# Rotary embedding on one core: the tail of a load as a DMA of its own, and the first store behind the rest of that load

## Chip, core and metric

The kernel runs on one core of a Trainium2 chip, with no other core of this program at work. The metric is the device time of one execution in microseconds (us).

## What is computed

A rotary position embedding. The input has 16 batches, 512 positions and 16 heads of 64 numbers, all float32. In each head the first half x1 and the second half x2 are turned by tables that depend on the position alone:

```python
# x: [16, 512, 16, 64]; cos, sin: [512, 32]
x1, x2 = x[..., :32], x[..., 32:]
out = concatenate([x1 * cos - x2 * sin,
                   x1 * sin + x2 * cos], axis=-1)   # float32
```

33.55 MB come in and 33.55 MB go out; the two tables have 64 KB each.

## The kernel before

**Slabs.** The work is cut into 8 slabs of 2 batches, 4.19 MB each: 8192 float32 (32 KB) on each of 128 partitions. Two neighbouring slabs are one stretch of HBM, and a partition's part of the two is one row of 64 KB, so a load or store of two slabs at once (k = 2) moves 64 KB per partition, one of a single slab 32 KB. The tile `room` has place for six slabs. Slabs 6 and 7 take the places of slabs 0 and 1.

**Loads and stores.** `loads` and `stores` say which slabs go alone and which in pairs:

```python
loads = {0: 1, 1: 1, 2: 2, 4: 2, 6: 1, 7: 1}
stores = {0: 1, 1: 1, 2: 1, 3: 1, 4: 2, 6: 1, 7: 1}
```

The loads of slabs 0, 1, 2-3 and 4-5 are issued on SP's DMA queue at the very start, one behind the other (L73). The tables come by ACT's queue (L89). The loads of slabs 6 and 7 are issued by ACT in the middle of its work, and each waits until the store whose place it takes (store 0, store 1) has landed. All seven stores go out on SP's queue (L182), each when the last pass over its slab is done. Hence store 0 is issued while the load of slabs 4-5 is still on its way, and its bytes stand behind that load's in the same queue.

**Compute.** TensorE spreads the tables over the partitions with eight small matmuls (L130), and VectorE (DVE) copies them to bfloat16 (L135). Each slab is then one pass of 8192 numbers per partition, or two passes of 4096 (slabs 0, 6 and 7). In a pass ScalarE (ACT) casts float32 to bfloat16 in place (`cast`, L146), DVE makes two products (L174) and their sum (L177), and ACT casts the result back to float32 in place (L178). ACT's cast of the next pass stands ahead of this pass's cast back.

**What sets the order.** ACT's and DVE's instructions keep the order in which the program writes them (`manual_schedule`); so does SP's queue in effect: four loads, then the stores 0, 1, 2, 3, 4-5, 6 and 7. Waits on semaphores are put in by the framework from the data that instructions share.

Of the kernel before, what the change touches and what calls it, by code (L numbers as in the profile page):

```python
# [2 lines left out]

# [4 lines left out]


@with_exitstack  # L10
def kernel(
    ctx: ExitStack,
    tc: tile.TileContext,
    x: bass.AP,
    cos: bass.AP,
    sin: bass.AP,
    num_heads: int,
    out: bass.AP,
):
    nc = tc.nc  # L20
    P = nc.NUM_PARTITIONS

    batch, seq, dim = x.shape
    nh = num_heads
    hd = dim // nh
    half = hd // 2
    bf16 = mybir.dt.bfloat16
    f32 = mybir.dt.float32

    nb = 2  # L30
    slots = 6
    LATE = 3
    nslabs = batch // nb
    G = 2
    rpp = nb * seq // P
    W = rpp * dim
    SP = seq // rpp
    TW = rpp * half

    out_flat = out.rearrange("b s h d -> b s (h d)")  # L40

    singles = ctx.enter_context(tc.tile_pool(name="singles", bufs=1))
    psum = ctx.enter_context(tc.tile_pool(
        name="psum", bufs=1, space=bass.MemoryType.PSUM))


    def dram(t, s, k):
        return bass.AP(tensor=t.tensor,
                       offset=t.offset + s // G * (G * nb * seq * dim) + s % G * W,
                       ap=[[G * W, P], [1, k * W]])  # L50


    def view(t, offset, *dims):
        return dataclasses.replace(t, offset=t.offset + offset,
                                   ap=[t.ap[0], *[list(d) for d in dims]])


    room = singles.tile([P, slots * W], f32, tag="room")
    halves = room.bitcast(bf16)


    def slab(s, k):
        return view(room, s % slots * W, (1, k * W))


    loads = {0: 1, 1: 1, 2: 2, 4: 2, 6: 1, 7: 1}
    stores = {0: 1, 1: 1, 2: 1, 3: 1, 4: 2, 6: 1, 7: 1}


    def load(s):  # L70
        k = loads[s]
        queue = nc.sync if s < slots else nc.scalar
        queue.dma_start(out=slab(s, k), in_=dram(x, s, k))  # L73

    TR = 32
    TQ = seq // TR // rpp
    TC = seq * half // TR
    raw = singles.tile([P, TC], f32, tag="raw")  # L80
    nc.vector.memset(raw, 0.0)  # L81


    def load_tables(queue):
        for i, src in enumerate((cos, sin)):
            to = dataclasses.replace(
                raw, offset=raw.offset + i * raw.ap[0][0],
                ap=[[P // TR * raw.ap[0][0], TR], [1, TC]])
            queue.dma_start(out=to, in_=bass.AP(  # L89
                tensor=src.tensor, offset=src.offset, ap=[[TC, TR], [1, TC]]))  # L90


    load(0)
    load_tables(nc.scalar)
    for s in loads:
        if 0 < s < slots:
            load(s)

    GP = SP // G
    GT = G // TQ
    pick = singles.tile([P, 3 * GT * P], bf16, tag="pick")
    nc.gpsimd.memset(pick, 0.0)  # L104


    def selection(g, h):
        return pick[:, (g * GT + h // TQ) * P:(g * GT + h // TQ + 1) * P]


    for g in range(3):
        for h in range(0, G, TQ):
            part = view(selection(g, h), 0, (GP, P // GP), (1, GP))
            nc.gpsimd.affine_select(  # L114
                out=part, in_=part, compare_op=mybir.AluOpType.not_equal,
                fill=-1.0 if g == 2 else 1.0,
                base=-(1 if g else 0) - h // TQ * (P // TR),
                pattern=[[0, P // GP], [-(G // TQ) * (P // TR), GP]],
                channel_multiplier=1)

    raw_b = singles.tile([P, TC], bf16, tag="raw_b")
    nc.gpsimd.tensor_copy(out=raw_b, in_=raw)  # L122

    tab = {}


    def table(h):
        acc = psum.tile([P, 2 * rpp * hd], f32, tag=f"acc{h}")
        for g, at in ((0, 0), (0, half), (2, rpp * hd), (1, rpp * hd + half)):
            nc.tensor.matmul(  # L130
                view(acc, at, (hd, rpp), (1, half)), selection(g, h),
                view(raw_b, h % TQ * TW, (half, rpp), (1, half)),
                start=True, stop=True)
        tab[h] = singles.tile([P, 2 * rpp * hd], bf16, tag=f"tab{h}", name="tab")
        nc.vector.tensor_copy(out=tab[h], in_=acc)  # L135

    def span(u):
        s, r, n = u
        at, m = s % slots * W + r * dim, n * dim
        return (m, view(room, at, (1, m)), view(halves, 2 * at, (1, m)),  # L140
                view(halves, 2 * at + m, (1, m)))


    def cast(u):
        m, full, low, high = span(u)
        nc.scalar.copy(out=low, in_=full)  # L146

    passes = []
    for s in range(nslabs):
        n = rpp if 1 <= s < nslabs - 2 else rpp // 2
        passes += [(s, r, n) for r in range(0, rpp, n)]


    with tc.manual_schedule(engines={mybir.EngineType.Activation, mybir.EngineType.DVE}):
        cast(passes[0])
        done = 1
        for i, u in enumerate(passes):  # L160
            s, r, n = u
            if i == 0:
                for h in range(G):
                    table(h)
            ahead = len(passes[:rpp // passes[0][2]]) if i == 0 else i + 1
            for v in passes[done:ahead + 1]:
                cast(v)
            done = max(done, ahead + 1)
            if s - LATE + slots in loads and s >= LATE and r == 0:
                load(s - LATE + slots)  # L170
            m, full, low, high = span(u)
            turned = view(low, half, (hd, n * nh), (-half, 2), (1, half))
            for out_, in_, a in ((high, turned, rpp * hd), (low, low, 0)):
                nc.vector.tensor_mul(  # L174
                    out=out_, in0=in_,
                    in1=view(tab[s % G], a + r * hd, (hd, n), (0, nh), (1, hd)))
            nc.vector.tensor_add(out=high, in0=low, in1=high)  # L177
            nc.scalar.copy(out=full, in_=high)  # L178
            if r + n == rpp:
                for t, k in stores.items():  # L180
                    if t + k - 1 == s:
                        nc.sync.dma_start(out=dram(out_flat, t, k), in_=slab(t, k))  # L182


# [1 line left out]
_INS = ['x', 'cos', 'sin', 'num_heads']  # L186
_OUTS = [((16, 512, 16, 64), 'float32')]

_NUMBERS = {'num_heads': 16}


# [26 lines left out]
```

## Time and profile before

| | us |
|---|---|
| median of 3 runs | 162.21 (162.21 to 162.39) |
| the profiled execution | 162.0 |
| its span in the profile | 160.2 |

| engine | busy in the span |
|---|---|
| VectorE (DVE) | 110.1 us (69%) |
| ScalarE (ACT) | 113.2 us (71%) |
| TensorE (PE) | 1.9 us (1%) |
| GpSimd (POOL) | 2.1 us (1%) |

Some events of the span, from the trace:

| us | what |
|---|---|
| 0.74 to 2.8 | SP issues the loads of slabs 0, 1, 2-3 and 4-5 |
| 13.3, 22.9, 42.2 | the loads of slabs 0, 1 and 2-3 have landed, and ACT's casts begin |
| 36.93 | SP issues store 0 |
| 56.19 | SP issues store 1 |
| 62.5 | the load of slabs 4-5 has landed |
| 72.28 | store 0 has landed; ACT issues the load of slab 6 |
| 88.01 | store 1 has landed; ACT issues the load of slab 7 |
| 139.6 | the last cast back ends; SP issues store 7 |
| 159.3 | store 7 has landed |

An instruction that issues a DMA ends long before its bytes have landed; "landed" is when the semaphore of the DMA has its full count. All DMAs, of whichever queue, are carried by the same 16 DMA engines. "Packets" are the pieces in which an engine carries a DMA; here a packet is one partition's part (32 or 64 KB), eight of them per engine and DMA.

### The profile page before, as it was taken

Reading aid. Unit: us, or ns where it says so; the run is one execution under the profiler, and the core shown is the slowest. Engines: PE = TensorE matmul, PEld = TensorE weight load, DVE = VectorE, ACT = ScalarE, POOL = GpSimd, SP = SyncE. Lnnn points to the kernel's source line nnn. Section 1 sums busy time; section 2 is a strip of 40 time slices with the busy share of each in tenths; the row PEclk is TensorE's granted clock in tenths of the full one; section 3 lists DMA queues with packets and bytes.
Section 4 is the critical chain, followed back from the end, with each engine's and each line's share of the span. In section 5 each row is a group of like instructions: output and inputs, shape, how many; then the busy total and the mean of one; then the engine's idle time right before and its main releaser. Section 6 shows DMA issues by size and latency. Waiting matters only on the chain.

```text
span 160.2 us, 170 instructions
## 1 busy us (share of the span) xinstructions
PE 1.9 (1%) x8; PEld 1.1 (1%) x8; DVE 110.1 (69%) x36; ACT 113.2 (71%) x23; POOL 2.1 (1%) x9
## 2 busy tenths in 40 slices
PE   0004000000000000000000000000000000000000
PEld 0002000000000000000000000000000000000000
DVE  1002999999906998999899899997399999000000
ACT  3006939992499999999999999299999991800000
POOL 3001000000000000000000000000000000000000
DMA  7999999979989996999999999999998998999994
GB/s 262 409 409 393 515 401 524 458 327 524 425 360 524 409 376 270 458 450 401 458 450 393 450 466 393 442 442 425 417 532 360 524 409 376 401 458 450 393 442 213
DMA packets 1968, 67.24 MB, mean 420 GB/s; under 512 B 240, under 2 KB 240, under 8 KB 304
## 3 DMA queue, kind: packets, MB, share of 16 engines
q1 hardware_dynamic: 1584, 58.72, 85.8%
q10 hardware_dynamic: 384, 8.52, 12.3%
HBM read 33.69 MB, written 33.55 MB: 420 GB/s over the span
## 4 chain that ended last, share of the span: by engine, by line
ACT 36%; DMA 25%; DVE 21%; issue 4%; SPq 1%; ACTq 0%
DMA room<-in_x_dram 25%; ACT room L178 20%; ACT room L146 17%; DVE room L174 14%; DVE room L177 7%; SPq L73 1%; ACTq L178 0%
## 5 line engine op out<-in xcount | busy, mean ns | idle before, releaser
L174 DVE TENSOR_TENSOR room<-room,tab 128x4096 bf16<-128x4096 bf16 (+1 forms) x22 | 71.7, 3260 | 10.9 <-ACT room L146 10.5
L146 ACT CAST room<-room 128x4096 bf16<-128x4096 f32 (+1 forms) x11 | 56.6, 5155 | 17.1 <-DMA room<-in_x_dram 17.1
L178 ACT CAST room<-room 128x4096 f32<-128x4096 bf16 (+1 forms) x11 | 56.6, 5156 | 6.6 <-DVE room L177 6.6
L177 DVE TENSOR_TENSOR room<-room 128x4096 bf16<-128x4096 bf16 (+1 forms) x11 | 35.9, 3262 | 0.4
L135 DVE CAST tab<-acc 128x1024 bf16<-128x1024 f32 x2 | 2.4, 1219 | 13.6 <-PE acc L130 13.6
L146 ACT ACT_TABLE_LOAD x1 | 1.3, 1283 | 2.6 <-issue 2.6
L130 PE MATMUL acc<-raw_b,pick 128*128 128x256 bf16 x8 | 1.9, 415 | 13.9 <-POOL raw_b L122 13.9
L130 PEld LDWEIGHTS <-pick 128*128 128x128 bf16 x8 | 1.1, 140 | 14.2 <-issue 12.3
L81 DVE MEMSET raw<- 128x512 f32 x1 | 0.5, 485 | 0.9 <-PEq L199 0.9
L114 POOL TENSOR_SCALAR_AFFINE_SELECT pick<-pick 128x128 bf16<-128x128 bf16 x3 | 0.8, 309 | 0.1
L122 POOL CAST raw_b<-raw 128x512 bf16<-128x512 f32 x1 | 0.6, 611 | 11.2 <-DMA raw<-in_sin_dram 11.2
L104 POOL MEMSET pick<- 128x384 bf16 x1 | 0.4, 418 | 0.3 <-POOLq L199 0.3
L199 POOL MEMSET const-float32-0.0<- 128x1 f32 x1 | 0.1, 99 | 0.2 <-issue 0.2
L199 POOL MEMSET const-bfloat16-1.0<- 128x1 bf16 x1 | 0.1, 102 | 0.0
L199 POOL MEMSET const-uint8-127<- 128x1 uint8 x1 | 0.1, 102 | 0.0
L199 POOL MEMSET const-float32-1.0<- 128x1 f32 x1 | 0.1, 99 | 0.0
## 6 DMA issues: line engine op xcount, KB each, us to landing
out_dram<-room SPq DMA_DIRECT2D x6, 4096.0 KB, 33.6
room<-in_x_dram SPq DMA_DIRECT2D x2, 4096.0 KB, 17.1
room<-in_x_dram ACTq DMA_DIRECT2D x2, 4096.0 KB, 24.8
raw<-in_cos_dram ACTq DMA_DIRECT2D x1, 64.0 KB, 7.9
raw<-in_sin_dram ACTq DMA_DIRECT2D x1, 64.0 KB, 11.1
room<-in_x_dram SPq DMA_DIRECT2D x2, 50.5
out_dram<-room SPq DMA_DIRECT2D x1, 28.7
```

Source lines behind the costliest of these rows:

```text
L73: queue.dma_start(out=slab(s, k), in_=dram(x, s, k))
L81: nc.vector.memset(raw, 0.0)
L104: nc.gpsimd.memset(pick, 0.0)
L114: nc.gpsimd.affine_select(out=part, in_=part, compare_op=mybir.AluOpType.not_equal, fill=-1.0 if g == 2 else 1.0, base=-(1 if g else 0) - ...
L122: nc.gpsimd.tensor_copy(out=raw_b, in_=raw)
L130: nc.tensor.matmul(view(acc, at, (hd, rpp), (1, half)), selection(g, h), view(raw_b, h % TQ * TW, (half, rpp), (1, half)), start=True, sto ...
L135: nc.vector.tensor_copy(out=tab[h], in_=acc)
L146: nc.scalar.copy(out=low, in_=full)
L174: nc.vector.tensor_mul(out=out_, in0=in_, in1=view(tab[s % G], a + r * hd, (hd, n), (0, nh), (1, hd)))
L177: nc.vector.tensor_add(out=high, in0=low, in1=high)
L178: nc.scalar.copy(out=full, in_=high)
L199: nc = _bacc.Bacc("TRN2", target_bir_lowering=False, num_devices=1)
```

## The change

The load of slabs 4-5 becomes two DMAs on the same queue, one behind the other: the first 56 KB of each partition (14336 numbers), then the last 8 KB (2048 numbers, `TAIL` = 2 rows of 1024; 1.05 MB in all). Store 0 gets a wait: SP issues it only when the first of the two has landed. SP's order is now written out too (`manual_schedule` names SP), and stays as it was: five loads, then the seven stores. Nothing else is changed.

```diff
     slots = 6
+    TAIL = 2
...
+    gates = {4: 0}
+    opened = {}
+
+    def piece(t, s, a, b):
+        return bass.AP(tensor=t.tensor,
+                       offset=t.offset + s // G * (G * nb * seq * dim) + s % G * W + a,
+                       ap=[[G * W, P], [1, b - a]])
 
     def load(s):
-        k = loads[s]
+        end = loads[s] * W
+        cut = end - TAIL * dim if s in gates else end
         queue = nc.sync if s < slots else nc.scalar
-        queue.dma_start(out=slab(s, k), in_=dram(x, s, k))
+        for a, b in ((0, cut), (cut, end)):
+            if a < b:
+                done = queue.dma_start(
+                    out=view(room, s % slots * W + a, (1, b - a)),
+                    in_=piece(x, s, a, b))
+                if s in gates and a == 0:
+                    opened[gates[s]] = done.ins
+
+    def store(s):
+        gone = nc.sync.dma_start(out=dram(out_flat, s, stores[s]), in_=slab(s, stores[s]))
+        if s in opened:
+            tc.add_manual_dep(
+                gone.ins, opened[s].name,
+                mybir.DependencyInfo(mybir.DependencyClass.Sync,
+                                     mybir.DependencyReason.DATA),
+                reason="behind the load")
...
-    with tc.manual_schedule(engines={mybir.EngineType.Activation, mybir.EngineType.DVE}):
+    with tc.manual_schedule(engines={
+            mybir.EngineType.Activation, mybir.EngineType.DVE, mybir.EngineType.SP}):
...
-                        nc.sync.dma_start(out=dram(out_flat, t, k), in_=slab(t, k))
+                        store(t)
```

## The prediction

> **What bounds the kernel now.** I read the DMA row of the page first, then the stage table of the trace, then the starts of packets around the one stage that stands out, and last SP's waits. The page says that the 16 DMA engines carry the run:
>
> ```profile
> DMA  7999999979989996999999999999998998999994
> ...
> HBM read 33.69 MB, written 33.55 MB: 420 GB/s over the span
> ```
>
> The DMA row is full from the second slice to the last but one, while DVE and ACT are busy 69% and 71% and are done by 139.6 us. All 67.24 MB at the rate of the best stages (434 GB/s) would be 154.9 us of the 160.2. On SP's queue the waits say the same of the stores (us in total, times, longest): each was held until ACT's last cast (L178) of its slab, and its bytes then waited for the DMA engines.
>
> ```profile
> SPq L182 <- ACT room L178: 123.8, 7, 27.0
> ```
>
>  The chain of waits names ACT and DVE for most of the span, but after 139.6 us it has no instruction left to name and 20 us of stores are still to come, so the chain isn't the bound; the DMA engines are. Where do they run below 434? The stage table, with stages cut where packets begin (last column GB/s, the one before it the DMA share):
>
> ```profile
> 22.00:41.40 19.40, 0.00 (x0) 0.00 (x0) 19.26 (x7) 14.04 (x3) 0.00 (x0) 1.00 1.00 432
> 41.40:58.30 16.90, 0.00 (x0) 0.00 (x0) 11.87 (x4) 16.08 (x3) 0.00 (x0) 1.00 1.00 434
> 58.30:61.55 3.25, 0.00 (x0) 0.00 (x0) 3.25 (x1) 3.25 (x1) 0.00 (x0) 1.00 1.06 323
> 61.55:71.20 9.65, 0.00 (x0) 0.00 (x0) 9.12 (x3) 9.65 (x3) 0.00 (x0) 1.00 1.01 435
> 71.20:86.90 15.70, 0.00 (x0) 0.00 (x0) 15.10 (x5) 15.70 (x3) 0.00 (x0) 1.00 1.00 434
> 86.90:114.00 27.10, 0.00 (x0) 0.00 (x0) 23.46 (x7) 24.07 (x5) 0.00 (x0) 1.00 1.01 437
> ```
>
> One stage sticks out: 58.30 to 61.55 us, 323 GB/s though the DMA share is 1. It is the last packet that each engine carries of the load of slabs 4-5, with store 0 next on the same queue. The starts of packets in 53 to 63 us show it (40 slices of 0.25 us; GB/s is put down to the slice in which a packet begins):
>
> ```profile
> DMA  0099000000099600000009900000000000999009
> GB/s 0 0 3146 1049 0 0 0 0 0 0 0 786 3146 262 0 0 0 0 0 0 0 2359 1835 0 0 0 0 0 0 0 0 0 0 0 524 655 918 0 0 786
> ```
>
> Weighted means of the starts: 56.09, 58.48, then 61.92. The steps are 2.39 and 3.44 us, where a 64 KB packet takes 2.42 (packet records): the last packets of the load are stretched by 1.02 us. The landings agree. Loads 2-3 and 4-5 have 8.39 MB each; load 1 landed at 22.85, loads 2-3 at 42.20 and 4-5 at 62.5 (issued at 2.1, 60.4 to landing), so 19.35 and then 20.3 us: 1.0 us more. Nowhere else between 3.8 and 158 us is a packet stretched like this; start-up (first packets at 1.75 to 2.25 us, 2 us instead of 1.2) and the end after 158 us aren't touched by the change. So about 1.0 us, 0.6% of the run, is what the edit can play for.
>
> **The change part by part.** The profiled execution took 162.0 us, of which 160.2 is span and 1.8 lies around it; it is 0.2 below the median of the three runs (162.21). The terms below are differences of span, and I put them on the median.
>
> *The split.* On each engine, 8 packets of 64 KB become 8 of 56 KB and 8 of 8 KB. No 8 KB or 56 KB packet is in the trace; the nearest records are 2 KB (0.084 us), 32 KB (1.213) and 64 KB (2.418). They fit 0.008 us per packet plus 27.2 GB/s, so 2.12 and 0.309 us: 16.94 + 2.48 = 19.42 against 19.34. The price is +0.07 us. It lies on the path, as every microsecond of the queue does, and it has no cover. From below it can't be under 0; from above, the 2 KB packets' rate (24.4 GB/s) for the whole tail would make it 0.27. The SP issue of one DMA more (0.4 us by the rows at 1.2 to 2.1 us) ends by 3.3 us, long before the queue needs it: nothing.
>
> *The new wait.* The last packets of loads 2-3 end at 41.57 (mean), so those of the first part of load 4-5 end at 41.57 + 16.94 = 58.5, and the tail's at 61.0. A landing counter follows the last packet by 0.3 us (62.2 to 62.5), and SP adds an EVENT_SEMAPHORE and its restart (0.1), so store 0 is issued at about 59.0, not at 36.93. What happens from issue to first byte? For a store on a drained queue no row shows it; load 0 is the nearest: issued at 0.74, its packets begin at 1.75 to 2.25 (1.0 to 1.5 us later), and end at 3.8 on the mean, which without the latency would be a flow from 2.6 (1.85 later). The same load from its landing: 12.6 us, less 9.65 for its bytes at 434.5 GB/s, 0.3 for the 0.13 MB of tables between and 0.3 for the counter, leaves 2.15. So store 0 stands in the queue from 60.1 to 60.5 and could flow from 60.9 to 61.2, where the tail ends at 61.0. The gap is 0 to 0.2 us; I take 0, since load 0's latency includes HBM reads and a store reads the SBUF. With a tail half as long the gap would be 1.2 us more: the tail is all the cover there is.
>
> [...]
>
> *The stretch.* Its cause isn't in a row; the place is. It lies on the last packet of a load while packets of a store stand behind it on the same queue. Load behind load (at 22 and 41.5 us) and store behind store (71, 139) go on at 432 to 435, and from 76.7 to 114 us loads on the ACT queue alternate with stores on SP's packet by packet at 434 to 437, so the change of direction by itself is cheap. What is left is a store read ahead while the load ahead of it on its queue is unfinished, and that needs store 0 to be queued early. After the change nothing of it is there until 60.3 (mean), 0.7 us before the tail ends. Taken from both ends: if all goes, −1.02; if all stays, 0. Some stretch may come back in those 0.7 us: before, 1.02 of 3.44 us were lost (30%), so 0.2. I take −1.02 + 0.2.
>
> *What is queued behind it.* On SP store 1 (data ready at 56.19, issued then) now stands behind the waiting store 0 and goes out at about 59.5. Its turn in the queue is after store 0's last packet, near 70.7: covered by 10 us. Store 2 (70.03) isn't touched. ACT's issue of load 6 waits for store 0's landing (72.26 now) and sits in ACT's order between a cast that runs from 69.91 to 76.93 and the next; anywhere in it, the wait costs ACT nothing. Load 7 lies likewise in the cast from 83.75 to 90.77. The listing of the changed kernel has the same order on SP and ACT and one more counter in use, so some waits name another counter, each of a DMA long landed. ACT reads slab 5, where the tail lies, from 83.75, 22 us after it lands. At the end compute is done at 139.6 and the last store's turn comes at 149.3, so a shift of a microsecond changes nothing but the queue: what is won or lost near 61 us reaches the end whole.
>
> Sum: 162.21 − 1.02 + 0.2 + 0.07 = 161.46, say 161.5 us.
>
> **The rivals.** *The stretch belongs to the first store itself*, wherever it starts: every engine's first write to HBM, or the one switch from load to store on a queue. For it: the trace has only this one such switch, so there is no second sample. Against it: the load's landing is late, not the store's first packet (store 0 lands 9.7 us after that landing, its bytes' time being 9.65). Then the store arrives under the tail, the tail or the first store packet is stretched instead, and the run is 162.21 + 0.07 = 162.3, no change that can be seen (162.0 to 162.5). [...]
>
> *The store comes late, and the switch costs as before.* This one ends slower. The gap is what the 2.48 us tail doesn't cover of counter, SP, descriptors and first bytes; I have 0.3 + 0.1 + 1.85 to 2.15, so 2.25 to 2.55, with nothing to spare. ACT's load 6 shows a slower start on a busy engine: issued at 72.28, first packet on its queue after 76.7, 4.4 us, three 1.21 us packets of the other queue among them, so 0.8 us of it is start. If the start of a store on a drained queue is 0.5 us over load 0's, the gap is 0.5 to 0.6, and with the stretch unrelieved the run is 162.21 + 0.07 + 0.5 = 162.8 (162.55 to 163.2). It decides from the point where gap and remaining stretch together pass 1.02 − 0.07 + 0.32 = 1.27 us.
>
> *The edit does nothing at its place*: the stretch is due to something else at 58 us, as SP's issue of store 1 at 56.19. Other issues (36.93, 70.03, 125.46) left no mark, so I give it little, and it gives the first rival's time.
>
> **How the numbers follow.** A difference under 0.2% (0.32 us) can't be told from none here: the three runs spread over 0.18. Forecast, the stretch goes for the most part: 0.48, 161.5, its own range 161.2 to 161.9. Stretch stays, no gap, the third rival included: 0.23, 162.3. Gap and stretch: 0.29, 162.8. Range 161.2 to 162.9: from nothing left of the stretch to somewhat over the second rival's middle. Faster 0.48, same 0.23, slower 0.29.
>
> **What would show it.** In the profile after, the first part's landing near 58.8 and SP's issue of store 0 near 59.0; the starts of packets in 53 to 63 us with steps of 2.1, then small packets from 58.5, and store 0's first packets at 61.0 to 61.3 instead of 61.92. Store 0 landing near 71.5, not 72.26, and every later landing earlier by as much; span near 159.5. The first rival shows store 0's packets at 61.9 to 62.0 with no empty slice. The second shows DMA slices empty around 61 us and the landing of store 0 past 72.5. The forecast is wrong if store 0's first packets begin after 61.6.

## The result, and the profile after

| | before | changed |
|---|---|---|
| median of 22 runs each | 162.21 us (161.98 to 162.39) | 162.93 us (162.18 to 163.64) |
| ratio | | 1.0040 (95% interval 1.0031 to 1.0050) |
| the profiled execution | 162.0 us, span 160.2 | 163.36 us, span 161.6 |

The change makes the kernel slower by 0.4%, 0.72 us at the median. The runs also spread wider, 1.46 us against 0.41. The profiled execution of the changed kernel is one of its slower ones; a second trace of it (below) has 162.84 us. In the numbers of the experiments, runs over 1.5% above the fastest of the same kernel are left out (164.63 and 164.77 us of one_queue_wait, 164.50 of pair_no_wait2).

At the place that the change aims at, it did all it is for. SP's waits (us in total, times, longest) have store 0 held by the load now; its timeline has the issue of stores 0 and 1 one behind the other:

```profile
SPq L93 <- ACT room L205: 77.8, 5, 27.0
SPq L93 <- DMA room<-in_x_dram: 55.8, 1, 55.8
...
59.29 0.82 SPq L93 DMA_DIRECT2D out_dram<-room  x2
```

The starts of packets in 53 to 63 us, slices of 0.25 us as in the prediction:

```profile
DMA  0005995000009990000007899997999993039900
GB/s 0 0 0 229 1835 1376 229 0 0 0 0 0 459 2294 918 0 0 0 0 0 0 295 361 426 393 459 524 328 393 459 393 1475 655 131 0 131 1311 655 0 0
```

The 56 KB packets begin every 2.1 us. The 8 KB packets follow from 58.3 and each takes 0.31 us. Store 0's first packets (the 1475, 655 and 131) begin from 60.75 to 61.25, straight behind the tail: no stretch, no empty slice between. Store 0 landed at 71.41 us, 0.85 earlier than before.

The loss comes back later. These are rows of the stage tables (last column GB/s), the kernel before first, then the changed one; the stage from 74 to 89 us is that in which ACT's load of slab 6 cuts in between the stores:

```profile
61.55:73.60 12.05, 0.00 (x0) 0.00 (x0) 11.49 (x4) 12.05 (x3) 0.00 (x0) 1.00 1.01 435
73.60:88.50 14.90, 0.00 (x0) 0.00 (x0) 14.33 (x4) 14.90 (x3) 0.00 (x0) 1.00 1.01 435
88.50:157.00 68.50, 0.00 (x0) 0.00 (x0) 42.49 (x16) 44.47 (x11) 0.00 (x0) 1.00 1.00 433
```

```profile
60.75:73.90 13.15, 0.00 (x0) 0.00 (x0) 12.58 (x4) 13.15 (x3) 0.00 (x0) 1.00 1.02 442
73.90:89.00 15.10, 0.00 (x0) 0.00 (x0) 14.53 (x4) 15.10 (x3) 0.00 (x0) 1.00 1.02 404
89.00:157.00 68.00, 0.00 (x0) 0.00 (x0) 42.03 (x16) 44.11 (x11) 0.00 (x0) 1.00 1.00 433
```

435 became 404 GB/s there, with the DMA share at 1: packets took longer, up to 2.55 us for 32 KB where the usual one takes 1.213. I measure this by an *excess*: the time of each packet record over 0.008 us plus its bytes at 27.2 GB/s, summed and divided by 16 engines (to about 0.03 us). Before, it is 1.02 us at 55 to 66 us and nothing after; changed, 0.02 at 55 to 66 and 1.32 after, on store packets near 75.4 us, and on load packets near 77 and from 84 to 87 us.

It is also uneven. The last stage, second by second (the first two rows are the kernel before, the other two the changed one):

```profile
158.00:159.00 1.00, 0.00 (x0) 0.00 (x0) 0.00 (x0) 0.00 (x0) 0.00 (x0) 1.00 0.01 0
159.00:160.20 1.20, 0.00 (x0) 0.00 (x0) 0.00 (x0) 0.00 (x0) 0.00 (x0) 1.00 0.00 0
```

```profile
158.00:159.00 1.00, 0.00 (x0) 0.00 (x0) 0.00 (x0) 0.00 (x0) 0.00 (x0) 1.00 0.31 131
159.00:160.20 1.20, 0.00 (x0) 0.00 (x0) 0.00 (x0) 0.00 (x0) 0.00 (x0) 1.00 0.07 27
```

Before, no packet of data begins after 158 us. In the changed kernel four begin between 158 and 159 (131 GB/s, four of 32 KB) and one after 159. By the records the 16 engines end at 158.72 us on the mean and 159.01 at the latest before, 159.14 and 160.41 after. The mean engine is 0.42 later and the last one 1.40, and the kernel ends with the last. That is the span's 1.35 us.

### The profile page after: what moved, and what is told of

Same layout as the page of the kernel before. It is cut to its first block, busy times and chain, and to the rows that moved or that the text cites. A ratio compares the mean times of both kernels' runs of the same rounds, so it can differ in the third digit from the quotient of the medians.

```text
span 161.6 us, 173 instructions
## 1 busy us (share of the span) xinstructions
PE 1.9 (1%) x8; PEld 1.1 (1%) x8; DVE 110.1 (68%) x36; ACT 113.3 (70%) x23; POOL 2.1 (1%) x9
## 4 chain that ended last, share of the span: by engine, by line
ACT 36%; DMA 25%; DVE 21%; issue 4%; SPq 0%; ACTq 0%
DMA room<-in_x_dram 25%; ACT room L205 20%; ACT room L172 16%; DVE room L201 14%; DVE room L204 7%; SPq L85 0%; ACTq L205 0%
```

## The experiments

Each was timed in turns with the kernel before on the same chip. "Excess" is that of the profiled execution, in us, from 3 to 66 us of the span and from there to its end.

| kernel | median us (range) | ratio to before (95%) | excess, 3 to 66 us / after |
|---|---|---|---|
| before | 162.21 (161.98 to 162.39) | | 1.03 / 0 |
| changed | 162.93 (162.18 to 163.64) | 1.0040 (1.0031 to 1.0050) | 0.06 / 1.32 |
| split_only | 162.14 (162.00 to 162.36) | 1.0001 (0.9992 to 1.0010) | 1.42 / 0 |
| wait_only | 164.79 (164.56 to 165.88) | 1.0180 (1.0154 to 1.0206) | 0.10 / 1.41 |
| tail3 | 162.44 (161.87 to 163.30) | 1.0016 (1.0000 to 1.0031) | 0.74 / 0.05 |
| tail4 | 162.16 (162.01 to 162.31) | 0.9998 (0.9989 to 1.0007) | 1.12 / 0 |
| store_head | 162.13 (162.04 to 162.33) | 0.9995 (0.9987 to 1.0004) | 1.19 / 0 |
| store0_on_act | 162.39 (162.26 to 162.56) | 1.0011 (1.0002 to 1.0019) | 1.31 / 0 |
| one_queue_wait | 162.82 (162.10 to 164.01) | 1.0051 (1.0026 to 1.0075) | 0.02 / 1.48 |
| one_queue_free | 162.78 (162.57 to 163.17) | 1.0041 (1.0029 to 1.0053) | 1.33 / 0.32 |
| three_waits | 162.21 (161.62 to 163.77) | 1.0007 (0.9984 to 1.0030) | 0.20 / 0.62 |
| pair_no_wait2 | 162.73 (162.05 to 163.77) | 1.0027 (1.0008 to 1.0046) | 0.55 / 1.35 |
| pair_free | 162.51 (162.30 to 162.78) | 1.0019 (1.0010 to 1.0028) | 1.37 / 0.18 |
| pair_wait | 161.61 (161.28 to 162.03) | 0.9963 (0.9950 to 0.9977) | 0.03 / 0.42 |

Up to 0.4 us of the first figure lies between 30 and 50 us in some traces (tail3, pair_no_wait2, pair_free), on packets of the load alone; no run here tells why. The nomix pair, which is shorter, has its times below.

The theory, M: an engine loses about 1 us where load and store packets first meet in it, once; a kernel that is spared this at the first store pays later.

### One half of the change at a time

```diff
-        if s in opened:            # split_only: store 0 waits for nothing but its data
+        if False and s in opened:
-    TAIL = 2                       # wait_only: no split, store 0 waits for the whole load
+    TAIL = 0
```

> The split stays, the wait goes: store 0 is issued at 37 us again and stands behind the 8 KB tail on SP's queue. Theory M (about 1 us is lost where load and store packets first meet in the DMA engines; the wait moves the meeting from 58 us to the first load on ACT's queue near 75 us, where it costs more and unevenly between engines): the meeting is back near 58 to 62 us, later packets are whole, time as before plus 0.1 for the split, 162.1 to 162.4. Rival S (the small packets or the fifth load make the run slower): slow as the changed kernel, 162.9, with stretched packets after 75 us.

> The wait stays, the split goes: store 0 waits for the whole load of slabs 4-5. M: no stretched packet at 58 us, an empty queue of 1.4 to 2.1 us after 61 us, and the same loss of 1 us or more after 75 us as in the changed kernel: 164.2 to 165.0. Rival S: the gap alone on top of before less the stretch, 162.6 to 163.3.

Starts of packets in split_only, 53 to 63 us:

```profile
GB/s 0 0 0 0 918 2294 459 0 0 0 0 0 0 2294 1376 0 0 0 0 0 0 33 426 426 164 295 229 98 295 164 328 131 197 262 459 393 1081 1180 131 0
```

The tail begins at full rate (426) and then falls to half, 100 to 330 a slice, until about 61.2 us. By the records its 8 KB packets take 0.31 us at first, about 0.6 in the slow part, and 0.31 again from 61.2 us on; store 0's first packets begin only after that, from 62.13 to 62.51. The fifth load and its small packets cost nothing that the timing can tell (ratio 1.0001); rival S falls. In wait_only the queue runs dry. A row of the stage between the load and the store, and SP's issue of stores 0 and 1:

```profile
61.00:62.20 1.20, 0.00 (x0) 0.00 (x0) 1.20 (x1) 1.20 (x1) 0.00 (x0) 1.00 0.00 0
61.66 0.82 SPq L93 DMA_DIRECT2D out_dram<-room  x2
```

Store 0 goes out at 61.66 us and its first packets begin at 62.5, 0.85 us later. The gap is 1.6 us in the mean of the engines, and the excess after 66 us (1.41) is that of the changed kernel. So the tail covers the gap in full, and the later loss comes with the wait, with or without a split. The time at which load 6 is issued doesn't explain it: 71.49 us in the changed kernel and 72.84 in wait_only, which have the loss, but 72.28 before and 72.63 in split_only, which haven't.

### No load after the first store

```diff
-            if s - LATE + slots in loads and s >= LATE and r == 0:
-                load(s - LATE + slots)
-    for s in range(nslabs):
+    for s in range(slots):
-                    if t + k - 1 == s:
+                    if t + k - 1 == s or (s == 3 and t >= slots):
```

> The kernel before without slabs 6 and 7 (their loads and arithmetic are left out, stores 6 and 7 send slabs 0 and 1 again, right after store 3), so that the queue carries loads up to 61 us and nothing but stores after. 8.4 MB less, 19.3 us: span near 140.9, time near 142.8. Both theories: one stretch of about 1.0 us at 58 to 62 us.

> The changed kernel without slabs 6 and 7 in the same way: no load comes after store 0. M: no stretched packet anywhere, 0.8 to 1.0 us faster than the same cut of the kernel before (near 141.9), and hardly any spread between runs. Rival S or any cost of the wait itself: as slow as that cut or slower.

142.98 us (142.86 to 143.09) and 141.67 (141.61 to 141.82): the change is worth 1.31 us here, more than the 0.8 to 1.0 expected, and the runs hardly spread. The stage of the last load packets, of nomix_before, and then three stages of nomix_after:

```profile
58.25:61.70 3.45, 0.00 (x0) 0.00 (x0) 3.45 (x1) 3.45 (x1) 0.00 (x0) 1.00 1.04 304
```

```profile
58.30:60.75 2.45, 0.00 (x0) 0.00 (x0) 2.45 (x1) 2.45 (x1) 0.00 (x0) 1.00 1.04 438
60.75:70.40 9.65, 0.00 (x0) 0.00 (x0) 9.12 (x3) 9.65 (x3) 0.00 (x0) 1.00 1.01 437
70.40:99.50 29.10, 0.00 (x0) 0.00 (x0) 27.97 (x7) 27.25 (x4) 0.00 (x0) 1.00 1.00 434
```

The mean engine ends 1.11 us earlier (138.33 instead of 139.44): the stretch of nomix_before, 1.16 us, is gone, less the price of the split. The last engine ends 1.33 earlier. So the gain is kept where no load comes after the stores have begun, and the wait as such costs nothing. The cut also leaves out the arithmetic of slabs 6 and 7 and sends their stores early. But compute is off the path, and the later loss of the changed kernel lies on packets of load 6 and on store packets just before them: what takes the gain away in the real kernel is the loads of slabs 6 and 7.

### When the store is queued

`TAIL = 3` and `TAIL = 4` in the changed kernel.

> The changed kernel with a tail of 12 KB per partition: store 0 is queued 1.2 us earlier against the end of the tail. M (paid once: what the first meeting of load and store packets doesn't cost near 60 us, a later one costs after 75 us): part of the stretch, 0.4 to 0.9 us, is back on the tail's packets, the excess after 75 us shrinks by as much or goes; 162.2 to 162.7. Rival P (the loss after 75 us belongs to a store issued late or to the wait, whatever the first meeting cost): the excess after 75 us stays at 1 us or more and adds to the stretch, 163.2 or more.

> A tail of 16 KB: store 0 is queued over 3 us before the tail ends. M: the whole stretch of 1.0 us is back on the tail, no stretched packet after 75 us, small spread between runs, 162.1 to 162.4. Rival P: 163.5 or more.

With 16 KB the stretch is back (3.40 us at 304 GB/s where tail4's last load packets lie) and the rest is clean:

```profile
58.20:61.60 3.40, 0.00 (x0) 0.00 (x0) 3.39 (x1) 3.40 (x1) 0.00 (x0) 1.00 1.03 304
71.30:157.00 85.70, 0.00 (x0) 0.00 (x0) 59.10 (x20) 61.67 (x13) 0.00 (x0) 1.00 1.01 434
```

With 12 KB the profiled run has 0.35 us on the tail and 0.05 later (another 0.39 us on the 52 KB packets at 43 to 50 us has no cause that I can name). So in this trace a partial meeting of 0.35 us left only 0.05 of later loss. The fixed sum of my theory doesn't hold here. But this trace is of one of its faster runs (162.12): over 12 runs the kernel ranges from 161.87 to 163.30, its median isn't below before's, and no trace shows what its slower runs pay. Rival P falls with both. In tail4 stores 0 and 1 are issued one behind the other too (56.84 us), so that isn't what costs later.

### Where the first meeting lies

```diff
-    gates = {4: 0}
+    gates = {}                               # both: no split of the load, no wait
+        cut = 2 * dim if s == 0 else end     # store_head: store 0 as 8 KB, then 24 KB
-        gone = nc.sync.dma_start(            # store0_on_act: store 0 on ACT's queue
+        queue = nc.scalar if s == 0 else nc.sync
+        gone = queue.dma_start(
```

> The kernel before, with store 0 as two DMAs: 8 KB per partition, then 24 KB; no wait, no split of the load. If the engines read ahead by packets (one store packet of 32 KB behind the last load packet, 1.2 us), the stretch falls to 0.3 us and either the time falls to 161.5 or a loss shows after 75 us. If they read ahead by bytes, the stretch stays 1.0 us and the time 162.2.

> The kernel before, with store 0 issued on ACT's queue at 37 us, so that its packets alternate with those of the load of slabs 4-5. Paid once, at the first meeting (M): an excess of about 1 us near 38 to 42 us and none later, 162.1 to 162.5. Rival Q (the price is that of a store behind a load on one queue): nothing near 40 us, 1.0 us where store 1 follows the load near 72 us, 162.1 to 162.5 too; the trace tells them apart. Both prices: 163.2.

A small first packet of the store changes nothing: 1.19 us of stretch, on the same last 64 KB packets. store0_on_act moves it. Store 0 is issued on ACT's queue near 37 us, and now the packets of loads that begin near 39 us are the stretched ones, in the middle of the load:

```profile
22.00:38.90 16.90, 0.00 (x0) 0.00 (x0) 16.80 (x6) 14.03 (x3) 0.00 (x0) 1.00 1.00 434
38.90:42.60 3.70, 0.00 (x0) 0.00 (x0) 3.67 (x2) 0.00 (x0) 0.00 (x0) 1.00 1.03 292
42.60:62.00 19.40, 0.00 (x0) 0.00 (x0) 11.69 (x4) 17.14 (x3) 0.00 (x0) 1.00 1.00 434
62.00:72.50 10.50, 0.00 (x0) 0.00 (x0) 9.97 (x3) 10.50 (x2) 0.00 (x0) 1.00 1.02 443
```

Near 72 us store 1 follows the load of slabs 4-5 on one queue with no stretch at all (443 GB/s up to 72.5 us, 439 from there to 84). Rival Q falls: the price here isn't that of a store behind a load on a queue, but that of the first store that an engine meets while loading.

### A second trace of the changed kernel

> The changed kernel once more, for a second trace: no stretch at 58 to 62 us, again 0.8 to 1.6 us of excess between 75 and 92 us, on other engines than in the first trace, 162.2 to 163.6.

162.84 us. No stretch at 58 to 62 us; 391 GB/s from 74 to 89 us and full rate after that:

```profile
74.00:89.00 15.00, 0.00 (x0) 0.00 (x0) 14.43 (x4) 15.00 (x3) 0.00 (x0) 1.00 1.01 391
89.00:157.00 68.00, 0.00 (x0) 0.00 (x0) 42.06 (x16) 44.03 (x11) 0.00 (x0) 1.00 1.00 433
```

The excess after 66 us is 1.55 us, more than in the first trace, yet the run is 0.5 us faster: here the last engine ends 0.39 us after the mean one (159.91 and 159.52), there 1.27. The packet records don't name their engine, so whether other engines were hit, as expected, isn't shown.

### Other orders of the loads and stores

All loads on SP's queue. In the one_queue kernels and three_waits they are behind stores 1 and 2; in the pair kernels both loads lie between stores 1 and 2.

```diff
-        queue = nc.sync if s < slots else nc.scalar
+        queue = nc.sync
-    LATE = 3                                  # one_queue_*, three_waits
+    LATE = 2
-            if s - LATE + slots in loads and s >= LATE and r == 0:   # pair_*
-                load(s - LATE + slots)
+            if s == 2 and r == 0:
+                load(6)
+                load(7)
-    gates = {4: 0}        # {} in *_free; {4: 0, 6: 2, 7: 3} in three_waits;
+    gates = {4: 0, 7: 2}  # this in pair_wait; {4: 0} in the other two
```

> The changed kernel with the loads of slabs 6 and 7 on SP's queue too, behind stores 1 and 2. M in its wide form (the meeting costs wherever load follows store): an excess of about 1 us where load 6 follows store 1, near 80 us, 162.5 to 163.2. In its narrow form (it costs where a second queue cuts in): no stretched packet anywhere, 161.0 to 161.5, and a kernel faster than both.

> The same one queue with neither split nor wait. Both forms of M: the stretch of 1.0 us at 58 to 62 us as in the kernel before and none later, 162.0 to 162.4; the wide form allows a second price at the later changes from store to load, up to 163.

> One queue as before, and every store that follows a load there waits for the first part of it: stores 0, 2 and 3 behind the loads of slabs 4-5, 6 and 7, each with an 8 KB tail. If a store queued too early is what costs (M), the excess of 1.0 us where store 2 follows load 6 (near 89 us) goes as that at 58 us went, and what is left is 0.3 to 0.5 us where loads follow stores (near 79 and 98 us): 161.5 to 162.0, below both kernels. If an engine has to pay about 1 us once whatever is queued (the price of reading ahead at all), the excess moves on to another place: 162.8 or more.

> All on SP's queue, loads 6 and 7 back to back between stores 1 and 2; stores 0 and 2 each wait for the first part of the load ahead of them (8 KB tails). One change from store to load is left. If each such change costs 0.3 us in the mean, as in the kernel with three waits, and a change from load to store with a late store nothing: an excess of 0.3 us near 80 us alone, 161.4 to 161.8, below both kernels. If the engines have to pay about 1 us whatever the order: 162.1 or more.

> The same without the wait of store 2, which then stands queued behind load 7 while that is on its way. A stretch of about 1.0 us near 96 to 100 us on the last packets of load 7, the 0.3 us near 80 us besides: 162.3 to 162.8.

> The order of pair_wait (all on SP's queue, loads 6 and 7 back to back between stores 1 and 2) with neither waits nor 8 KB tails. If the waits make the gain: the stretch of 1.0 to 1.3 us at 58 to 62 us is back, little or nothing later, 162.2 to 162.6. If the order alone makes it: 161.6.

one_queue_wait has 0.31 us of excess near 79 us, where load 6 follows store 1, and 1.07 from 87.7 to 92 us, where store 2, queued early, follows load 6. So most of the loss stands at a change from load to store, not where the wide form of M had it. In one_queue_free the stretch at 58 us is back and these two places have 0 and 0.21; its 162.78 us is above the 162.4 that was expected without a later price. In three_waits the latter is gone, and what is left, 0.62 us, lies near 79 and 99 us where loads follow stores. Its best run is 161.62 us, but the median is 162.21 and the worst 163.77, so on the median that expectation was missed. pair_wait leaves one change from store to load. Its stages (the second is that change):

```profile
60.75:78.70 17.95, 0.00 (x0) 0.00 (x0) 16.89 (x5) 17.95 (x4) 0.00 (x0) 1.00 1.00 434
78.70:82.70 4.00, 0.00 (x0) 0.00 (x0) 3.96 (x2) 4.00 (x1) 0.00 (x0) 1.00 0.97 385
82.70:98.00 15.30, 0.00 (x0) 0.00 (x0) 14.74 (x4) 15.30 (x4) 0.00 (x0) 1.00 1.00 429
98.00:157.00 59.00, 0.00 (x0) 0.00 (x0) 33.50 (x14) 34.94 (x9) 0.00 (x0) 1.00 1.01 437
```

Its median is 161.61 us, 0.37% below before (0.9963, 0.9950 to 0.9977), with 0.30 us of excess near 79 to 82 us and 0.03 near 98: a kernel faster than both. Without the second wait it is 162.73, with a new excess of 0.72 us at 98 to 101 us, and with 0.6 near 79 to 83 us, where pair_wait, the same program up to there, has 0.30: that loss varies between runs. Without either wait it is 162.51, with the stretch of 58 to 62 us back (1.09 us). So in this order, with one change from store to load left, the waits make the gain. In the one_queue order, with two such changes, the kernel with three waits is 0.6 us below the one without (162.21 and 162.78), and the kernel with one wait isn't (162.82).

## Why the prediction was wrong

**The split.** +0.07 us was forecast; the 8 KB packets took 0.309 us as worked out, and split_only can't be told from before. Right.

**The wait and its cover.** Issue of store 0 forecast at 59.0, measured 59.29; first packets forecast at 61.0 to 61.3, measured 60.75 to 61.25; landing forecast near 71.5, measured 71.41. No gap was forecast and none is there. In wait_only, where the queue was drained, store 0 began 0.85 us after its issue, a little sooner than load 0's 1.0 to 1.5, which was the bound; 1.4 us pass there from the end of the load's last packet (61.13) to store 0's first (62.51), where the second rival added up 2.25 to 2.55. Whether it starts sooner because it reads the SBUF, as the prediction has it, no run shows. Two of the prediction's figures for the start of a DMA were misread: load 0's landing leaves 12.6 − 9.65 − 0.3 − 0.3 = 2.35 us, not 2.15, and the first packet of load 6 began at 76.10, not after 76.7, so that only about 0.2 of its 3.8 us is start. Neither changed the outcome.

**The stretch.** −1.02 with 0.2 coming back was forecast; all of it went (0.02 left at 55 to 66 us), and nothing came back there.

**What is queued behind it.** Store 1 was covered as forecast. Slab 6's cast came to wait for its load (97.87 us, 2.6 later than before) by 0.15 us, far off the path: compute still ended near 139.6 us.

**The step that failed** is the last one before the sum: "what is won or lost near 61 us reaches the end whole". It rests on the sentence that loads alternate with stores at 434 to 437 GB/s from 76.7 to 114 us, "so the change of direction by itself is cheap". That row was true, but of engines that had met loads and stores together at 58 us already. It was no proof that the alternation is cheap for engines that hadn't: in the changed kernel the first 15 us of that stage run at 404. The kernels whose engines had lost their 1 us by then (before, split_only, tail4, store_head, store0_on_act) have no excess after 66 us; those that were spared it (changed, its second trace, wait_only) have 1.3 to 1.55. The term missing from the sum is that excess after 74 us, and up to 1 us more for the engine that ends last. The nomix pair, in which that term can't fall due, gains 1.31 us; the sum without its 0.2 had 0.95, and the stretch was 1.16 there, not 1.02.

**The rivals.** The one that ended slower gave 162.8, near the 162.93 measured, but by luck, not for its reason: there was no gap, and the stretch was relieved. The first rival had the price tied to the first store "wherever it starts"; nomix_after has a first store without any price, so it isn't that either. The range ended at 162.9, 0.03 us below the median. It had room for a late store, none for a second meeting of loads and stores.

**Open.** The runs show when the price falls due, not what it is. That it is bytes of a store read ahead while a load is being written is a conjecture, here as in the prediction. It fits the runs: the tail's packets go at half rate for some 2.4 us while store 0 stands behind and at full rate again before it begins (split_only), as if only so much were read ahead, and 1.0 to 1.3 us at 27.2 GB/s would be 27 to 35 KB per engine, by my estimate. But no run here looks inside an engine. Why the later loss differs so much between engines and runs, and why the one trace with 12 KB of tail escapes most of both, stays open too.

## What to carry to other kernels

A full-rate stage shows what a pattern costs in the state in which that stage found the machine: from 74 to 89 us load 6 and the stores went at 435 GB/s in the kernel before and at 404 in the changed one. Before a stall is taken out, ask what later stage may run well because of it, and look for a cut of the kernel in which that later stage is missing: here it gave −1.31 us where the whole gave +0.72. Here 16 engines shared the DMAs and the slowest set the end (160.41 us, the mean 159.14), so look at the spread of their last packets beside the mean rate.

## What the runs showed of the hardware

The first time that a store was queued while an engine was loading, about 1 us per engine was lost: 1.0 to 1.3 at that place in the eight traces where store 0 was issued about 5 us or more before the load's end (1.02 in the kernel before, 1.16 in nomix_before, 1.31 in store0_on_act), 0.35 where it waited for all but the last 12 KB of the load (tail3). It made no difference which queue the store was on (1.31 on ACT's, store0_on_act), or whether its first packet had 8 or 32 KB (1.19 in store_head, 1.02 before).

After that, loads from ACT's queue and stores from SP's alternated at 434 GB/s with nothing lost (before, tail4). On one queue, each later change from load to store took 0.1 to 0.2 us, those from store to load nothing (in all 0.32 in one_queue_free, with two changes of each kind, and 0.18 in pair_free, with one).

A store that waited for all but the last 8 KB of the load was next to free there: 0.02 us of excess in the changed kernel, where it was issued 1.7 us before the load's end (59.29 and 61.0), and 0.03 near 98 us in pair_wait. Engines that began to store that way, or after the whole load, lost 0.3 to 0.6 us at a later change from store to load on one queue (0.31 in one_queue_wait, 0.30 in pair_wait, 0.6 in pair_no_wait2), 0.7 to 1.1 where a later store was queued early behind a load (0.72 in pair_no_wait2, 1.07 in one_queue_wait), and 1.3 to 1.55 us in all when loads came in from a second queue (1.32 in the changed kernel, 1.55 in its second trace, 1.41 in wait_only).
